# Decoder block on one core: gate recurrence between two heads, PEER routing kept on VectorE, fused W-block instructions, last V products by column halves

## The chip, the core and the metric

One core of a Trainium2 chip runs the whole kernel. Engines are named as in the profile: PE (TensorE matmul) and PEld (its weight load), DVE (VectorE), ACT (ScalarE), POOL (GpSimd) and SP (SyncE, which here only issues DMAs). The metric is the device time of one execution in microseconds, the median of the runs shown.

## What is computed

One decoder layer over 512 tokens of width 1024, in float32 (one layer, one batch):

```python
h = rmsnorm(x, norm1_w) * (1 + sc1) + sh1            # modulated by c @ ada_w
qa, ka, va, qm, km, vm, om, ip, fp, ga, gm = split(h @ w_in)
y_a = diff_attention(rope(qa), rope(ka), va, ...)    # 8 heads
hm  = mlstm_chunkwise(conv(qm), conv(km), vm, ip, fp)  # 8 heads, stabilised gates
merged = sigmoid(ga) * y_a + sigmoid(gm) * (rmsnorm(hm) * sigmoid(om))
x  = x + gt1 * (merged @ w_out)
h2 = rmsnorm(x, norm2_w) * (1 + sc2) + sh2
# PEER: 8 heads, each with two half queries against 128 keys
v_top, i_top = top_k(q @ sub_keys, 16)               # both halves
cand = v_top[0][:, None] + v_top[1][None, :]         # 16 x 16
sc, sel = top_k(cand, 16); idx = (i_top[0] * 128 + i_top[1])[sel]
y = sum_e softmax(sc)[e] * gelu(U[idx[e]] . h2) * V[idx[e]]    # 16384 experts
x = rmsnorm(x + gt2 * y, final_norm_w)
```

Only candidates (i, j) with (i+1)(j+1) <= 16 can be among the best 16, so each head has 50 candidates in rows of 16, 8, 5, 4, 3, 2, 2, 2 and eight single ones (`PAIRS`, `NC` = 50).

## The kernel before

Float32 products are made of three float32r products, hi*hi, hi*lo and lo*hi: `split` (L135) rounds on ACT and subtracts on DVE or POOL, and every weight goes through it.

**Mixers** (`attention`, L443, `mlstm`, L513, called from the loop over four head pairs at L667). A head pair's projections are PE work with two PSUM banks (`acc`); attention of its two heads follows, then `mlstm`, with the projections of `om`, `gm` and `ga` around them. For the first pair `gate_chain` (L331) stands between `attention` and `mlstm`: the running sums and running maxima of the gates of all heads (`tensor_tensor_scan` on DVE, L347 and L349, in 8 partitions), three Exp on ACT (L355 to L357), bf16 thirds copied by ACT and POOL (L363, L364), and the transposes that give `RT`. Its tiles `M` and `iw` lie in the ring `t2k` of three buffers, which rope and attention's output `oT` use too.

**Routing** (from L710). Token tile 0 (`GB`) goes by gathers, tiles 1 to 3 (`DBS`) densely. `scores(h)` projects one head's queries and takes the top 16 of each half (`top16`, five DVE instructions). `select` (L772) works on four heads of one token tile. Its old form builds the candidate sums `cand` on DVE and the candidate indices `cidx` on POOL, takes their top 16, and then finds each pick's index head by head: a 16x50 comparison `eq` on DVE (L797), its product `oh` with `cidx` on POOL (L799), a sum on DVE (L800). `slots` (L816) transposes indices and gates and splits an index into its two key numbers. `build_w` (L833) makes, for 8 tokens at a time (48 blocks), two one-hot tiles and two gated tiles of 128x1024 in float16 with the helper `each` (L843), all on DVE but for the last gated tile of every eighth block, which POOL makes (`PLO`); 16 float16 matmuls (L852, L853) then give the block of W, which ACT evacuates and writes to DRAM.

**Dense loop** (from L984). For key row n1, `up(n1)` (L961) loads a 128x1024 block of U (SP), rounds it (ACT), makes its low part at L967 (POOL for n1 < 35, DVE from there), and runs 24 matmuls (L975 to L977); the result waits in one of 32 `ga` buffers (`NGA`). The loop then multiplies by W (L1006), splits, and runs 18 matmuls against the V block (L1021) into six PSUM banks `ys[d][j]`, d the token tile and j the column half. The last three blocks of V are multiplied together, d by d. In `up`, gathers for token tile 0 are released on POOL behind a small copy, `pace` (L969); `select_gather` runs `select` on its eight heads at n1 = 3 and 5. The end (L1033) scales, adds x, normalises and stores tile by tile.

**What sets the order.** Each engine runs its instructions in one fixed order. It is laid down when the kernel is built, by a scheduler that gives a free engine the ready instruction that stands earliest in the program, and hands out tile buffers as they come free. So the 32 possible `up` calls run ahead into the time in which W is built: they depend on nothing in it, but stand behind it in the program.

Of the kernel before, what the change touches and what calls it, by code (L numbers as in the profile page):

```python
# [61 lines left out]
def block_kernel(ctx: ExitStack, tc: tile.TileContext, a, out, dbg=None):  # L62
# [380 lines left out]
    def attention(hp, y, ssq):  # L443
# [283 lines left out]
    iota_c = dp.tile([P, NC], F16, name="iota_c")  # L727
# [44 lines left out]
    def select(vals, inds, n, mk, didx, dgate):  # L772
# [5 lines left out]
        cidx = mk("cidx", [P, n, NC])  # L778
        for eng, dst, src in ((V, cand, vals), (G, cidx, fi)):
            off = 0  # L780
            for i in range(8):
                m = PAIRS[i]
                eng.tensor_tensor(dst[:, :, off:off + m], src[:, 1, :, 0:m],
                                bc(src[:, 0, :, i:i + 1], [P, n, m]), op=OP.add)
                off += m
            eng.tensor_tensor(dst[:, :, off:off + 8], src[:, 0, :, 8:16],
                            bc(src[:, 1, :, 0:1], [P, n, 8]), op=OP.add)
# [21 lines left out]
    def mk_rp(name, shape, dt=F32):  # L809
        return rp.tile(shape, dt, tag=name, bufs=2, name=name)  # L810
# [298 lines left out]
```

## Time and profile before

| | us |
|---|---|
| median of 3 runs (1979.67 to 1980.06) | 1979.73 |
| the profiled execution | 1986.29 |
| its span, first to last instruction | 1984.2 |
| PE, PEld, DVE, ACT, POOL busy in the span | 1826.5, 1648.0, 1465.3, 806.8, 861.2 |

The busy time of an engine counts overlapping instructions once. Matmuls are pipelined, so that the time of one is longer than the distance to the next. In the views by stretch, PEclk is the granted clock of PE as a share of its higher level, 2.4 GHz (the lower is 1.2 GHz). Mixers end near 640 us, scores run to about 770 us, W is built from 808 to 1005 us, the dense loop ends at 1972 us.

### The profile page before, as it was taken

How to read it: one execution, taken by the hardware profiler on the slowest of the kernel's cores; microseconds unless marked ns; L12 is line 12 of the kernel's file. 1: busy time of each engine (PE TensorE's matmuls, PEld its weight loads, DVE VectorE, ACT ScalarE, POOL GpSimd, SP SyncE). 2: the span in 40 equal slices, each digit the busy share in tenths (PEclk: the TensorE clock that was granted, in tenths of full speed). 3: DMA queues.
4: the chain of work that ended last, by engine and by line, in shares of the span. 5: the costliest groups of instructions: out<-in, count | busy, mean ns of one | idle time of the engine just before them, and what ended most of it. 6: DMA issues, size and time to landing. Idle time of an engine off the chain costs nothing.

```text
span 1984.2 us, 29045 instructions
## 1 busy us (share of the span) xinstructions
PE 1826.5 (92%) x10748; PEld 1648.0 (83%) x10748; DVE 1465.3 (74%) x2740; ACT 806.8 (41%) x1361; POOL 861.2 (43%) x721
## 2 busy tenths in 40 slices
PE   5989999899997988778899989999999999999997
PEld 4979899798986877678888778889988888888986
DVE  7653646546557799998999878888777677767777
ACT  4545464464553323344444333333333333332332
POOL 2513425234234256675533556555433423333433
PEclk8999999999998999899899999999999999999998
DMA  7321414324223222255596699999978888887983
GB/s 278 123 64 60 149 65 154 113 67 139 64 86 107 86 90 81 85 183 202 203 312 215 216 331 339 334 345 348 337 253 296 293 283 291 288 299 234 320 290 129
DMA packets 160284, 404.27 MB, mean 204 GB/s; under 512 B 14471, under 2 KB 63368, under 8 KB 160142
## 3 DMA queue, kind: packets, MB, share of 16 engines
q1 hardware_dynamic: 117026, 240.91, 37.2%
q0 software_dynamic: 36864, 134.23, 18.6%
q10 hardware_dynamic: 6252, 27.28, 3.6%
q8 instruction: 84, 1.38, 0.3%
q14 instruction: 58, 0.48, 0.1%
HBM read 373.52 MB, written 28.84 MB: 203 GB/s over the span
## 4 chain that ended last, share of the span: by engine, by line
PE 51%; DVE 23%; DMA 10%; issue 6%; POOL 5%; ACT 4%; SPq 0%; DVEq 0%; POOLq 0%; ACTq 0%
PE y L1021 18%; PE act L977 5%; PE act L975 5%; PE act L976 5%; DMA ada_w<-ada_w 4%; DMA gath<-V,idx 3%; DVE onehot L844 3%; DVE gated L844 2%; DVE lo_V L138 1%; DVE lo_U L967 1%; DVE eq L797 1%; DMA gath<-U,idx 1%; POOL gath L901 1%; DVE idxf L800 1%; ACT hi_U L966 1%
## 5 line engine op out<-in xcount | busy, mean ns | idle before, releaser
L977 PE MATMUL act<-h_hi,lo_U 128*128 128x384 f32 x1024 | 353.9, 346 | 14.7 <-POOL lo_U L967 9.7
L975 PE MATMUL act<-h_hi,hi_U 128*128 128x384 f32 x1024 | 351.5, 343 | 1.9 <-ACT ga L979 1.9
L976 PE MATMUL act<-h_lo,hi_U 128*128 128x384 f32 x1024 | 350.7, 342 | 0.0
L917 DVE SCALAR_TENSOR_TENSOR yg<-gath,act,yg 128x1024 f32<-128x1024 f32 x127 | 162.9, 1283 | 110.3 <-DMA gath<-V,idx 109.6
L1021 PE MATMUL y<-lo_V,ahi 128*128 128x512 f32 x762 | 238.9, 394 | 5.5 <-DVE lo_V L138 5.5
L1021 PE MATMUL y<-hi_V,alo 128*128 128x512 f32 x762 | 234.1, 394 | 4.0 <-DVE alo L138 4.0
L1021 PE MATMUL y<-hi_V,ahi 128*128 128x512 f32 x762 | 222.1, 396 | 7.3 <-ACT hi_V L137 7.3
L901 POOL DMA_INDIRECT gath<-U,idx x128 | 176.6, 1380 | 115.3 <-DVE junk L907 101.1
L137 ACT CAST hi_V<-raw_V 128x1024 fp32r<-128x1024 f32 x128 | 134.1, 1051 | 225.6 <-PE y L1021 197.1
L977 PEld LDWEIGHTS act<-h_hi,lo_U 128*128 128x128 f32 x1024 | 197.0, 192 | 22.4 <-POOL lo_U L967 11.1
L969 POOL COPY pace<-lo_U 128x1 f32<-128x1 f32 x128 | 69.9, 548 | 331.6 <-DVE lo_U L967 330.1
L975 PEld LDWEIGHTS act<-h_hi,hi_U 128*128 128x128 f32 x1024 | 197.8, 193 | 10.8 <-ACT ga L979 3.1
L976 PEld LDWEIGHTS act<-h_lo,hi_U 128*128 128x128 f32 x1024 | 197.5, 193 | 3.6
L137 ACT CAST ahi<-ga 128x384 fp32r<-128x384 f32 x127 | 65.1, 513 | 302.2 <-DVE ga L1006 152.1
L138 DVE TENSOR_TENSOR lo_V<-raw_V,hi_V 128x1024 fp32r<-128x1024 f32 x128 | 158.0, 1236 | 33.2 <-ACT hi_V L137 30.6
L966 ACT CAST hi_U<-raw_U 128x1024 fp32r<-128x1024 f32 x128 | 134.1, 1048 | 110.0 <-PE act L976 92.3
L1021 PEld LDWEIGHTS y<-hi_V,alo 128*128 128x128 f32 x762 | 143.5, 189 | 35.9 <-DVE alo L138 5.2
L1021 PEld LDWEIGHTS y<-lo_V,ahi 128*128 128x128 f32 x762 | 142.7, 189 | 36.7 <-DVE lo_V L138 7.9
L1021 PEld LDWEIGHTS y<-hi_V,ahi 128*128 128x128 f32 x762 | 143.0, 190 | 32.1 <-ACT hi_V L137 8.0
L901 POOL DMA_INDIRECT gath<-V,idx x128 | 152.5, 1192 | 38.0 <-issue 30.2
L907 DVE SCALAR_TENSOR_TENSOR junk<-gath,hrow 128x1024 bf16<-128x1024 f32 x128 | 156.1, 1220 | 11.9 <-DMA gath<-U,idx 11.2
L967 POOL TENSOR_TENSOR lo_U<-raw_U,hi_U 128x1024 fp32r<-128x1024 f32 x35 | 105.0, 3001 | 72.5 <-ACT hi_U L966 59.1
(461 smaller groups left out, 4413.1 us busy)
## 6 DMA issues: line engine op xcount, KB each, us to landing
raw_U<-UT SPq DMA_DIRECT2D x128, 512.0 KB, 5.1
raw_V<-V SPq DMA_DIRECT2D x128, 512.0 KB, 5.0
ada_w<-ada_w SPq DMA_DIRECT2D x96, 256.0 KB, 4.0
W_dram<-st ACTq DMA_DIRECT2D x24, 960.0 KB, 4.5
W<-W_dram SPq DMA_DIRECT2D x60, 384.0 KB, 10.4
raw_wq<-wq SPq DMA_DIRECT2D x16, 512.0 KB, 3.5
raw_q<-w_in SPq DMA_DIRECT2D x8, 512.0 KB, 4.9
raw_k<-w_in SPq DMA_DIRECT2D x8, 512.0 KB, 3.6
```

The costliest lines, as they stand in the source:

```text
L137: A.copy(hi, src)
L138: eng.tensor_tensor(lo, src, hi.bitcast(F32), op=OP.subtract)
L844: eng.tensor_tensor(dst.rearrange("p t (n u) -> p t n u", u=2), x.rearrange("p t (n u) -> p t n u", u=2), bc(y[:, b * TB:(b + 1) * TB, Non ...
L901: G.indirect_dma_start(out=t_, out_offset=None, in_=src, in_offset=bass.IndirectOffsetOnAxis(ap=idx0[:, s:s + 1], axis=0))
L907: V.scalar_tensor_tensor(junk2, u, 1.0, hrow, op0=OP.mult, op1=OP.mult, accum_out=act[:, s:s + 1])
L917: V.scalar_tensor_tensor(yg, v, act[:, s:s + 1], yg, op0=OP.mult, op1=OP.add)
L966: A.copy(hi, raw)
L967: (G if n1 < NGA + 3 else V).tensor_tensor(lo, raw, hi.bitcast(F32), op=OP.subtract)
L975: T.matmul(ps, hi[:, ks], h_hi[:, k], start=(k == 0), stop=False)
L976: T.matmul(ps, hi[:, ks], h_lo[:, k], start=False, stop=False)
L977: T.matmul(ps, lo[:, ks], h_hi[:, k], start=False, stop=(k == KD - 1))
L1021: T.matmul(ys[d][j], l[:, tsl], r[:, j * 512:(j + 1) * 512], start=(m == 0 and i == 0), stop=(m == KEYS - 1 and i == 2))
```

## The change

- `gate_chain` is called at the start of the second head of the first pair, between the two heads, instead of behind `attention`.
- `select` no longer uses POOL. The 50 candidate positions are decoded into row and column without a table of 50: a float16 comparison of each position with the 16 row starts (`off_c`), products with the differences of the row indices and of the row starts, one sum over both, and a second comparison and sum for the column. Four heads share each instruction. It returns the two key numbers apart, so that `slots` needs no shift and mask; it transposes three tiles instead of two.
- `build_w` makes both one-hot tiles of a block in one instruction, and both gated tiles in another (128x2048 each), always on DVE.
- The low parts of all U blocks are made on DVE.
- In the last V products, each token tile first runs all products of column half 0, then those of half 1.

```diff
-    def attention(hp, y, ssq):
+    def attention(hp, y, ssq, between=None):
...
         for u in range(2):
+            if u and between:
+                between()
...
-        attention(hp, y_a, ssq[:, 0])
-        if hp == 0:
-            gate_chain()
+        attention(hp, y_a, ssq[:, 0], gate_chain if hp == 0 else None)
...
+    n21T = rp.tile([P, XT // TB, 2, TB, 2], F16, name="n21T")
+    ghl = rp.tile([P, XT // TB, 2, TB, 2], F16, name="ghl")
...
+    iota_rep = bc(iota16[:, None, :], [P, 2 * TB, KEYS])
+    V.tensor_copy(iota_c, jcol[:, 0:TOPK])
+    for i in range(TOPK):
+        G.memset(off_c[:, i:i + 1], float(OFFS[i]))
+        G.memset(doff_c[:, i:i + 1], float(OFFS[i] - OFFS[max(i - 1, 0)]))
...
-        fi = mk("fi", [P, 2, n, TOPK])
-        A.activation(fi[:, 0], inds[:, 0], AF.Copy, scale=float(KEYS))
-        A.copy(fi[:, 1], inds[:, 1])
+        ij = mk("ij", [P, 2, n, TOPK], F16)
+        A.copy(ij, inds)
+        di = mk("di", [P, n, TOPK], F16)
+        V.tensor_copy(di[:, :, 0:1], ij[:, 0, :, 0:1])
+        V.tensor_tensor(di[:, :, 1:], ij[:, 0, :, 1:], ij[:, 0, :, :TOPK - 1], op=OP.subtract)
...
-        for h in range(n):
-            eq, oh = mk("eq", [P, TOPK, NC], F16), mk("oh", [P, TOPK, NC])
-            sh = [P, TOPK, NC // 2, 2]
-            V.tensor_tensor(eq.rearrange("p k (c u) -> p k c u", u=2), bc(pos2[:, h, :, None, :], sh),
-                            bc(iota_c.rearrange("p (c u) -> p c u", u=2)[:, None], sh), op=OP.is_equal)
-            G.tensor_tensor(oh, eq, bc(cidx[:, h, None, :], [P, TOPK, NC]), op=OP.mult)
-            V.tensor_reduce(didx[:, h], oh, axis=AX.X, op=OP.add)
+        sh = [P, n * TOPK, TOPK // 2, 2]
+        sh4 = [P, n, TOPK, TOPK]
+
+        def each_pos(dst, table, op):
+            V.tensor_tensor(dst.rearrange("p q (c u) -> p q c u", u=2), bc(pos2[:, :, None, :], sh),
+                            bc(table.rearrange("p (c u) -> p c u", u=2)[:, None], sh), op=op)
+
+        def of_head(dst, src, table):
+            V.tensor_tensor(dst.rearrange("p (h k) c -> p h k c", h=n), src.rearrange("p (h k) c -> p h k c", h=n),
+                            bc(table[:, :, None, :], sh4), op=OP.mult)
+        ge = mk("ge", [P, n * TOPK, TOPK], F16)
+        st = mk("stp", [P, 2 * n * TOPK, TOPK], F16)
+        two = mk("two", [P, 2, n * TOPK])
+        each_pos(ge, off_c, OP.is_ge)
+        of_head(st[:, 0:n * TOPK], ge, di)
+        V.tensor_tensor(st[:, n * TOPK:], ge, bc(doff_c[:, None, :], [P, n * TOPK, TOPK]), op=OP.mult)
+        V.tensor_reduce(two.rearrange("p a q -> p (a q)"), st, axis=AX.X, op=OP.add)
+        V.tensor_copy(dn1, two[:, 0].rearrange("p (h k) -> p h k", k=TOPK))
+        V.tensor_tensor(pos2, pos2, bc(two[:, 1, :, None], [P, n * TOPK, 2]), op=OP.subtract)
+        eq = mk("ge", [P, n * TOPK, TOPK], F16)
+        each_pos(eq, iota_c, OP.is_equal)
+        of_head(eq, eq, ij[:, 1])
+        V.tensor_reduce(dn2, eq.rearrange("p (h k) c -> p h k c", h=n), axis=AX.X, op=OP.add)
...
-            each(e2, iota_rep, n2T, OP.is_equal)
-            each(e1, iota_rep, n1T, OP.is_equal)
-            each(r_hi, e1, ghi, OP.mult)
-            each(r_lo, e1, glo, OP.mult, G if b % 8 < PLO else V)
+            V.tensor_tensor(pairs[0].rearrange("p a t (n u) -> p (a t) n u", u=2),
+                            iota_rep.rearrange("p t (n u) -> p t n u", u=2),
+                            bc(n21T[:, b].rearrange("p a t u -> p (a t) u")[:, :, None, :], [P, 2 * TB, KEYS // 2, 2]),
+                            op=OP.is_equal)
+            V.tensor_tensor(pairs[1].rearrange("p a t (n u) -> p a t n u", u=2),
+                            bc(e1.rearrange("p t (n u) -> p t n u", u=2)[:, None], [P, 2, TB, KEYS // 2, 2]),
+                            bc(ghl[:, b][:, :, :, None, :], [P, 2, TB, KEYS // 2, 2]), op=OP.mult)
...
-        (G if n1 < NGA + 3 else V).tensor_tensor(lo, raw, hi.bitcast(F32), op=OP.subtract)
+        V.tensor_tensor(lo, raw, hi.bitcast(F32), op=OP.subtract)
...
+            steps = [(j, m, i, l, r) for m, ahi, alo, vhi, vlo in vparts
+                     for i, (l, r) in enumerate(((ahi, vhi), (ahi, vlo), (alo, vhi))) for j in range(2)]
+            if n1 == KEYS - 1:
+                steps.sort(key=lambda s: s[0])
+            for j, m, i, l, r in steps:
+                T.matmul(ys[d][j], l[:, tsl], r[:, j * 512:(j + 1) * 512],
+                         start=(m == 0 and i == 0), stop=(m == KEYS - 1 and i == 2))
```

## Rows read from the trace of the kernel before

**Rows 1.** The page: busy us, share of the span, instructions of each engine.
```profile
PE 1826.5 (92%) x10748; PEld 1648.0 (83%) x10748; DVE 1465.3 (74%) x2740; ACT 806.8 (41%) x1361; POOL 861.2 (43%) x721
```
**Rows 2.** Stretches: us, busy (x) of PE, PEld, DVE, ACT, POOL; PEclk, DMA share, GB/s.
```profile
130.00:160.00 30.00, 17.59 (x83) 14.25 (x84) 17.09 (x45) 16.52 (x39) 5.09 (x4) 0.72 0.12 40
...
690.00:808.00 118.00, 98.70 (x482) 86.90 (x482) 111.44 (x573) 40.25 (x73) 72.38 (x92) 0.94 0.28 87
808.00:1005.00 197.00, 163.00 (x1333) 153.21 (x1332) 182.65 (x217) 85.37 (x144) 119.59 (x61) 0.91 0.52 183
1005.00:1200.00 195.00, 183.79 (x884) 160.03 (x882) 172.43 (x410) 70.95 (x101) 89.40 (x77) 0.98 0.80 269
1200.00:1950.00 750.00, 740.03 (x3671) 663.86 (x3670) 565.47 (x680) 259.37 (x355) 331.10 (x305) 1.00 0.86 300
```
**Rows 3.** Waits of PE in the whole span: for whom, us, times, longest.
```profile
PE wps L852 <- DVE gated L844: 17.0, 8, 5.2
...
PE pt_gm L187 <- ACT om L682: 6.6, 1, 6.6
```
**Rows 4.** One stretch, one line each: L844 (DVE, POOL), L797 (DVE), L783 (DVE, POOL).
```profile
690.00:1005.00 315.00, 166.53 (x186) 15.69 (x6) 0.92 0.43 147
...
690.00:1005.00 315.00, 24.13 (x24) 0.92 0.43 147
...
690.00:1005.00 315.00, 12.43 (x48) 9.41 (x48) 0.92 0.43 147
```
**Rows 5.** DVE's timeline: start, us, what.
```profile
802.41 0.57 DVE L797 TENSOR_TENSOR eq<-pos,iota_c 128x800 f16<-128x800 f16 x1
802.89 0.21 DVE L805 TENSOR_REDUCE esm<-ex 128x4 f32<-128x64 f32 x1
...
843.88 2.88 DVE L844 TENSOR_TENSOR onehot<-iota,n2T 128x1024 f16<-128x1024 f16 x1
...
859.67 0.68 DVE L844 TENSOR_TENSOR gated<-onehot,ghi 128x1024 f16<-128x1024 f16 x1
860.27 0.68 DVE L844 TENSOR_TENSOR gated<-onehot,glo 128x1024 f16<-128x1024 f16 x1
...
1043.60 1.13 DVE L783 TENSOR_TENSOR s<-room 128x64 f32<-128x64 f32 x8
```
**Rows 6.** POOL's timeline at the same time as DVE's long one-hot.
```profile
843.32 2.89 POOL L967 TENSOR_TENSOR lo_U<-raw_U,hi_U 128x1024 fp32r<-128x1024 f32 x1 [1.12 <-ACT hi_U L966]
```
**Rows 7.** Lines L967 and L800: ns min/median/max, first and last start us, form.
```profile
L967 DVE TENSOR_TENSOR lo_U<-raw_U,hi_U x93: 1199/1222/1228, 1040.4 to 1945.0; 128x1024 fp32r<-128x1024 f32 x93
...
L967 POOL TENSOR_TENSOR lo_U<-raw_U,hi_U x35: 2340/2562/8862, 751.1 to 1014.3; 128x1024 fp32r<-128x1024 f32 x35
...
L800 DVE TENSOR_REDUCE idxf<-oh x24: 958/970/980, 722.3 to 873.6; 128x16 f32<-128x800 f32 x24
```
**Rows 8.** Stretches, line L976 alone (8 matmuls of each up call): PE, PEld.
```profile
690.00:808.00 118.00, 21.60 (x60) 12.82 (x61) 0.94 0.28 87
808.00:1005.00 197.00, 69.01 (x190) 39.22 (x190) 0.91 0.52 183
```
**Rows 9.** PE's timeline within one up call.
```profile
826.88 0.33 PE L976 MATMUL act<-h_lo,hi_U 128*128 128x384 f32 x1
827.05 0.34 PE L977 MATMUL act<-h_hi,lo_U 128*128 128x384 f32 x1
```
**Rows 10.** The gate recurrence: DVE's and ACT's timelines.
```profile
141.65 0.46 DVE L349 TENSOR_TENSOR_SCAN M<-Gr,mprev 8x128 f32<-8x128 f32 x1
...
149.58 0.61 ACT L355 ACTIVATE iw<-iw 8x512 f32<-8x512 f32 x1
...
152.13 1.08 ACT L682 ACTIVATE om<-pt_om 128x512 f32<-128x512 f32 x2
```
**Rows 11.** The end: PE's last product and DVE's last instruction.
```profile
1971.19 0.63 PE L1021 MATMUL y<-hi_V,ahl 128*128 128x512 f32 x2
...
1979.30 1.41 DVE L1046 SCALAR_TENSOR_TENSOR W<-W,ssq,fw 128x512 f32<-128x512 f32 x2 [0.66 <-POOL ssq L119]
```

More of the change, by code (lines that the diff above doesn't have):

```diff
@@ L37 @@
 NC = sum(PAIRS)
+OFFS = [sum(PAIRS[:i]) for i in range(TOPK)]
 PIECES = [c for hp in range(4) for c in (
@@ L726, in block_kernel @@
     jcol = dp.tile([P, KEYS], I32, name="jcol")
-    iota_c = dp.tile([P, NC], F16, name="iota_c")
+    off_c, doff_c, iota_c = [dp.tile([P, TOPK], F16, name=n) for n in ("off_c", "doff_c", "iota_c")]
     w0pool = ctx.enter_context(tc.tile_pool(name="w0", bufs=1, side="right"))
@@ L770, in scores, with select @@
         A.dma_start(s0_dram[:, h], s0)
-    def select(vals, inds, n, mk, didx, dgate):
-        fi = mk("fi", [P, 2, n, TOPK])
-        A.activation(fi[:, 0], inds[:, 0], AF.Copy, scale=float(KEYS))
-        A.copy(fi[:, 1], inds[:, 1])
-        cand = mk("cand", [P, n, NC])
[L778 to L787, printed above, removed]
+    def select(vals, inds, n, mk, dn1, dn2, dgate):
+        ij = mk("ij", [P, 2, n, TOPK], F16)
[3 more added lines that the diff above has]
+        V.tensor_tensor(di[:, :, 1:], ij[:, 0, :, 1:], ij[:, 0, :, :TOPK - 1], op=OP.subtract)
+        cand = mk("cand", [P, n, NC])
+        off = 0
+        for i in range(8):
+            m = PAIRS[i]
+            V.tensor_tensor(cand[:, :, off:off + m], vals[:, 1, :, 0:m], bc(vals[:, 0, :, i:i + 1], [P, n, m]), op=OP.add)
+            off += m
+        V.tensor_tensor(cand[:, :, off:off + 8], vals[:, 0, :, 8:16], bc(vals[:, 1, :, 0:1], [P, n, 8]), op=OP.add)
         sc = mk("scs", [P, n, TOPK])
@@ L809, in mk_rp @@
     def mk_rp(name, shape, dt=F32):
[L810 removed]
+        return rp.tile(shape, dt, tag=name, bufs=1 if name == "stp" else 2, name=name)
     def select_dense(t, h0, n):
         hs = slice(h0, h0 + n)
[L814 removed]
+        select(vals[t][:, :, hs], inds[t][:, :, hs], n, mk_rp, *[picks[t][:, i, hs] for i in range(3)])
     def slots(t):
[L818 removed]
+        bs = slice((t - DBS[0]) * P // TB, (t - DBS[0] + 1) * P // TB)
         ps = tr_tile("slots")
[L820 to L831 removed]
+        for i in range(3):
+            T.transpose(ps[:, i * P:(i + 1) * P], picks[t][:, i].rearrange("p h k -> p (h k)"), ident)
+        for i in range(2):
+            src = ps[:, i * P:(i + 1) * P].rearrange("p (b t) -> p b t", t=TB)
+            V.tensor_copy(n21T[:, bs, 1 - i], bc(src[:, :, :, None], [P, P // TB, TB, 2]))
+        gp = bc(ps[:, 2 * P:3 * P].rearrange("p (b t) -> p b t", t=TB)[:, :, :, None], [P, P // TB, TB, 2])
+        V.tensor_scalar(ghl[:, bs, 0], gp, GS, None, op0=OP.mult)
+        V.scalar_tensor_tensor(ghl[:, bs, 1], gp, GS, ghl[:, bs, 0], op0=OP.mult, op1=OP.subtract)
     def build_w(t):
[L836 removed]
         for b in range((t - DBS[0]) * P // TB, (t + 1 - DBS[0]) * P // TB):
@@ L926, in mk @@
             n = int(np.prod(shape[1:])) * (2 if dt == F16 else 4) // 4
[L927 removed]
+            if name in ("ge", "stp"):
                 t_, n0 = gpool.tile([P, D], F32, tag="g", bufs=NGB, name=name), 0
[L929 to L930 removed]
+            elif name == "cand":
+                t_, n0 = s0, 0
             else:
@@ L1017, in block_kernel @@
             tsl = slice(d * P, (d + 1) * P)
-            for m, ahi, alo, vhi, vlo in vparts:
-                for i, (l, r) in enumerate(((ahi, vhi), (ahi, vlo), (alo, vhi))):
-                    for j in range(2):
-                        T.matmul(ys[d][j], l[:, tsl], r[:, j * 512:(j + 1) * 512],
-                                 start=(m == 0 and i == 0), stop=(m == KEYS - 1 and i == 2))
+            steps = [(j, m, i, l, r) for m, ahi, alo, vhi, vlo in vparts
[5 more added lines that the diff above has]
+                         start=(m == 0 and i == 0), stop=(m == KEYS - 1 and i == 2))
         vparts = []
```

38 lines of the change are left out of this document (7 added, 31 removed).

## The prediction

> **What bounds the kernel now.** First the page's busy shares: PE is the busiest engine over the span, 92%, DVE second with 74% [rows 1]. The shares are means over stages, so I read the busy times by stretch next [rows 2]. From 1200 to 1950 us PE is busy 740 of 750 us at a granted clock of 1.00: there only less PE work would help, and the change removes none. Three places are different. From 690 to 1005 us PE is busy 98.7 + 163.0 = 261.7 of 315 us, at a clock of 0.94 and 0.91, while DVE is busy 111.4 + 182.7 = 294.1: this stage waits for DVE. From 130 to 160 us PE is busy 17.6 of 30 us at 0.72. And the end: PE's last product ends at 1971.8 us, DVE's last instruction at 1980.7 [rows 11], 9 us in which PE has nothing to do. Then the waits of PE say what ends the idle time: 17.0 us for gated tiles of W, 6.6 us in a single wait for `om` [rows 3]. So the question for each part is how much PE idle time it takes out, and how much PE work it pushes later.
>
> **W stage: why DVE is slow there.** The 186 one-hot and gated instructions on DVE take 166.5 us [rows 4], 0.90 us each. One undisturbed has 0.68 us, and the next starts 0.60 us after it; one at 843.88 takes 2.88 us, and POOL's lo_U runs from 843.32 for 2.89 us [rows 5, 6]. At 0.60 us the 186 would need 112 us: 55 us are lost while POOL computes. The change takes from POOL all that it computes in this stage but the small copies: lo_U, oh, cidx, the gated tiles.
>
> **The sum for DVE, 690 to 1005 us.** I use the distance to the next start, since durations overlap by 0.08 us.
> - W: 96 fused instructions of 2048 elements. 800 elements take 0.48 us to the next start and 1024 take 0.60 [rows 5], so 2048 take 0.60 + 1024 x 0.12/224 = 1.15 us, if the fused form keeps that rate; 110.4 us in place of 166.5: -56.1. Fusing itself gives only 2 x 0.60 - 1.15 = 0.05 us an instruction; the rest is POOL's absence.
> - lo_U: 35 move from POOL to DVE, which makes the other 93 in 1.22 us [rows 7], 1.14 to the next start: +39.9 (a few fall behind 1005 us).
> - Select, six dense groups: old, 24 comparisons in 24.1 us [rows 4] and 24 sums of 0.97 us [rows 7], 47.4 us, or 43.5 without overlaps. New per group: five float16 instructions of 1024 elements at 0.60 = 3.0; four small ones at 0.2, as the reduction of 64 elements (0.21 us) [rows 5]; two sums. A sum of 800 float32 takes 0.97 us [rows 7] and one of 64 0.21 [rows 5], that is 0.00103 us an element, so 1024 take 1.12 and 2048 2.17 us to the next start. Together 7.1 us, 42.6 for six: -1.
> - The candidate sums: 12.4 us for six groups [rows 4], against 1.13 us a group later in the trace [rows 5]: -5.6.
>
> In all -56.1 + 39.9 - 1 - 5.6 = **-23 us** of DVE. Of the sums over float16 no row exists: at the rate of the float16 comparisons they would be 1.15 and 0.60 us, 9 us less over six groups; I take the float32 rate, since it is the same operation, and keep 9 us for the lower end. The Trainium skill (VectorE: DVE Perf Modes, "The perf-mode tier table (the rule you actually need)") says that tensor_reduce has only the one-element mode, whatever the type; by that rule the stage stays at -23, by the other rate it would be -32. No row before shows which.
>
> The stage shortens by less than DVE's 23 us: PE needs 262 of the 315 us, and the two wait for each other block by block. With 17 us gone PE would be 88% busy, still under its 99% in the dense loop. I take **-17**, with 0 and -32 as bounds.
>
> What else moves: oh and cidx on POOL vanish; nothing waits for POOL there then but the pace copies. 32 memsets of one column go to POOL ahead of the scores, hidden in its idle time (72 of 118 us busy from 690 on [rows 2]); without that cover some 0.2 us each, taken from the nearest small DVE row, 6 us, and select alone would wait. A third transpose for each of three token tiles replaces shift and mask: nothing. The two selects for gathers, from 1005 to 1200 us, cost DVE about the same as before; DVE is 88% busy there [rows 2], and PE's dense products hide it. No DMA is added, and SP's queue is as before.
>
> **Gate recurrence.** The first running maximum starts at 141.65 us, right behind the second head's last split, and the Exps that need it (149.58) stand on ACT ahead of the sigmoid of `om` (152.13) [rows 10]. That sigmoid frees the PSUM bank for which `gm`'s projection waits 6.6 us [rows 3]. Called between the heads, the chain stands earlier on both queues, and `om`'s sigmoid need no longer queue behind it. Between 130 and 160 us PE does 17.6 x 0.72 = 12.7 us of full-clock work, so at most 17.3 us can be won (the clock, between its levels of 1.2 and 2.4 GHz here, fell after PE's waits). Against that, 16 short and 2 longer DVE instructions, about 6 us, now stand in front of the second head's maxima, and whoever waits for these, Exp, transposes and value products, starts later; PE has `om`, `gm` and `ga` to fill in. I take **-10**, bounds -17 and +6.
>
> **The end.** Half 0 of the last token tile is complete nine products earlier: 0.17 us for 384 columns [rows 9] makes 0.23 for 512, so 2 us, and its scaling, addition and square run beside half 1's products. I take **-2**, bounds -3 and 0.
>
> **Sum.** -17 - 10 - 2 = -29 us. The profiled execution took 1986.29 us, 6.6 above the median of 1979.73; I subtract from the median: 1951 us.
>
> **Rivals.**
> - *The up calls starve (slower).* lo_U now stands in DVE's queue behind W, which is earlier in the program. 250 matmuls of eight a call [rows 8] say that 31 up calls are done by 1005 us, 24 of them since 808. Each one fewer costs PE later 24 matmuls at 0.17 us [rows 9] = 4.1 us, and relieves DVE by 1.14: net 3.0. From ten fewer on all gains are gone; 18 fewer give 1951 + 54 = 2005 us. For it: DVE is the full engine, and W feeds it without a break. Against it: the index sums of the later token tiles ran until 873.6 us [rows 7], among W's blocks, though they stand behind W's first 16 blocks in the program, so W left room. Chance 0.14.
> - *DVE's time is won, the stage's is not.* If PE and DVE wait for each other in turn, only the 6 us of candidate sums ahead of W remain: 1979.7 - 6 - 12 = 1962 us. For it: PE waits 17.0 us in eight waits [rows 3], few for so long a stage; against it, 55 us of lost DVE time lie on a chain that PE waits for. Chance 0.2.
> - *The recurrence delays the second head:* +6 for -10, 1967 us. Chance 0.1.
> - *The fused instruction does not keep its rate*, because of its wider broadcast. At lo_U's rate (1.14 for 1024) 2048 elements take 2.2 us, 96 x 1.05 = +101: about 2050 us. Against it: pairs of equal values stay the innermost dimension, as in the rows at 0.68. Chance 0.03.
>
> **The numbers.** The forecast has 0.53: 1951 us, its own range 1932 to 1958. A measurement of this kernel tells about 0.2%, 4 us, from no change. Faster: 0.53 + 0.2 + 0.1 less 0.02 = 0.81; within 4 us 0.03, a starving of about ten calls; slower 0.16. For the range, all lower bounds together give -32 - 17 - 3 = -52, 1928, and 3 more for the clock that W's stage would get back: 1925. Upwards it takes in both half gains and the mild starving, to 1982; beyond lie some 0.13 of starving and the lost rate, below 0.04.
>
> **What would show it.** Right: in the W stage the DVE rows at 1.15 to 1.25 us for 2048 elements with no long ones, lo_U on DVE among them, about 30 up calls done when the last block of W is, and that moment 15 to 25 us earlier. PE's wait for `om` gone, and the stretch from 130 to 160 us full at clock 1.00. The last DVE instruction 6 to 7 us after PE's last product in place of 9. Wrong: up calls bunched behind W's last block, W's instructions over 2 us, or PE idle for the second head's maxima near 130 us.

## The result and the profile after

The changed kernel takes 1932.1 us (1931.4 to 1935.7) against 1979.9: a ratio of 0.976 [0.974, 0.978], 47.8 us less. The forecast was 1951, so the direction was right and the gain too small by 19 us. The time is inside the range, at the lower edge of the forecast's own 1932 to 1958.

The page of the profile after, busy time of each engine, beside [rows 1]:

```profile
PE 1814.8 (94%) x10751; PEld 1632.7 (85%) x10751; DVE 1430.7 (74%) x2700; ACT 812.5 (42%) x1359; POOL 691.2 (36%) x608
```

POOL lost 170 us of work; DVE, which took over the larger part of it (lo_U and gated rows), is 35 us *less* busy. The stretches show where. First the same columns as in [rows 2] for the gates and for the whole routing and W stage, from the first query product of the router to the last W block; then its last two parts:

```profile
130.00:160.00 30.00, 26.04 (x201) 23.85 (x200) 16.92 (x28) 22.58 (x44) 12.52 (x8) 1.00 0.23 75
...
625.00:959.00 334.00, 309.17 (x2185) 283.90 (x2185) 310.27 (x906) 151.44 (x258) 77.75 (x82) 0.96 0.47 160
...
812.00:931.00 119.00, 119.00 (x1069) 114.85 (x1067) 115.22 (x117) 67.96 (x115) 38.09 (x21) 1.00 0.67 234
931.00:960.00 29.00, 17.10 (x193) 14.90 (x192) 26.82 (x24) 16.25 (x28) 9.07 (x1) 0.76 0.69 260
```

The same stage of the kernel before, in the same view:

```profile
637.00:1006.00 369.00, 312.86 (x2120) 285.31 (x2120) 336.91 (x951) 146.88 (x258) 208.71 (x163) 0.92 0.41 139
```

The stage went from 369 to 334 us, and PE's idle time in it from 56.1 to 24.8. It also holds more work now. The groups of PE, the third product of each up call (8 a call), before and after:

```profile
L977 PE MATMUL act<-h_hi,lo_U 128*128 128x384 f32 x251 | 92.8, 370 | 9.7 <-POOL lo_U L967 9.7
```
```profile
L994 PE MATMUL act<-h_hi,lo_U 128*128 128x384 f32 x272 | 93.7, 345 | 2.5 <-DVE lo_U L984 2.5
```

That is 31 calls by the last W block before, 34 after; the mean of one product fell from 370 to 345 ns as the granted clock rose from 0.92 to 0.96. From 812 to 931 us PE is full at 1.00, where it was busy 163.0 of 197 us at 0.91 before [rows 2]; from 931 on it has no up call left (34 is all that there is room for, 32 in `ga` buffers and two in PSUM banks) and waits for W.

PE's waits in the stage before (us, times, longest), beside the 17.0 us of [rows 3]:

```profile
PE act L977 <- POOL lo_U L967: 9.7, 5, 4.3
PE slots L820 <- DVE idxf L800: 6.0, 1, 6.0
PE wps L853 <- POOL gated L844: 5.2, 2, 3.6
PE pkeys L764 <- DVE scr L749: 4.9, 1, 4.9
PE wps L853 <- DVE gated L844: 4.2, 5, 1.8
```

And what is left after:

```profile
PE wps L868 <- DVE gated L863: 10.0, 9, 2.5
PE act L992 <- ACT ga L996: 5.2, 3, 2.8
PE act L994 <- DVE lo_U L984: 2.5, 3, 0.9
```

DVE's groups in that stage after (busy us and mean ns, then the idle time ahead of them):

```profile
L859 DVE TENSOR_TENSOR onehot<-iota,n21T 128x2048 f16<-128x2048 f16 x48 | 57.5, 1217 | 2.7 <-PE wps L869 2.4
L863 DVE TENSOR_TENSOR gated<-onehot,ghl 128x2048 f16<-128x2048 f16 x48 | 57.4, 1215 | 0.1
L984 DVE TENSOR_TENSOR lo_U<-raw_U,hi_U 128x1024 fp32r<-128x1024 f32 x36 | 43.6, 1212 | 1.4 <-ACT hi_U L983 1.1 <-issue 0.2
...
L815 DVE TENSOR_REDUCE two<-stp 128x128 f32<-128x2048 f16 x6 | 13.6, 2264 | 0.0
...
L821 DVE TENSOR_REDUCE picks<-ge 128x64 f32<-128x1024 f16 x6 | 7.2, 1201 | 0.0
```

None of these means is more than 0.02 us above what the forecast took for an undisturbed instruction; before, the first one-hot alone had 1067 ns for 1024 elements, and DVE waited 12.6 us for PE ahead of it:

```profile
L844 DVE TENSOR_TENSOR onehot<-iota,n2T 128x1024 f16<-128x1024 f16 x48 | 51.0, 1067 | 12.6 <-PE wps L853 12.6
```

**Where the time went.** Three marks cut every execution: Q, the start of the second head pair's first query product; W, the end of the last W block; and the end of the span. This table holds for all that follows (medians with lowest and highest; ratios, with 95% intervals, to runs of the kernel before that were measured beside each kernel; the last three columns from the profiled execution):

| kernel | us | ratio | to Q | Q to W | W to end |
|---|---|---|---|---|---|
| before | 1979.9 | 1 | 180 | 826 | 978 |
| after | 1932.1 (1931–1936) | 0.976 [0.974, 0.978] | 167 | 791 | 971 |
| after, gates back | 1953.5 (1950–1955) | 0.987 [0.984, 0.990] | 180 | 788 | 981 |
| after, lo_U on POOL | 1938.8 (1936–1940) | 0.979 [0.976, 0.983] | 168 | 802 | 968 |
| after, four instructions | 1926.6 (1921–1933) | 0.974 [0.971, 0.978] | 165 | 795 | 960 |
| after, POOL work ahead of W | 1951.5 (1949–1953) | 0.985 [0.982, 0.989] | 170 | 812 | 970 |
| before, gates moved | 1970.3 (1965–1975) | 0.996 [0.993, 0.998] | 165 | 826 | 977 |
| before, lo_U to DVE | 1961.5 (1958–1965) | 0.992 [0.990, 0.994] | 181 | 804 | 975 |
| after, POOL work beside W | 1972.8 (1968–1977) | 0.998 [0.996, 1.000] | 166 | 833 | 968 |
| after, old column order | 1932.9 (1927–1937) | 0.978 [0.973, 0.983] | 169 | 792 | 969 |
| after, old select | 1943.6 (1940–1954) | 0.983 [0.978, 0.988] | 165 | 801 | 972 |
| after, 35 buffers | 1914.3 (1913–1919) | 0.966 [0.962, 0.970] | 169 | 795 | 953 |
| the same, four instructions | 1921.4 (1919–1923) | 0.970 [0.966, 0.974] | 169 | 802 | 949 |
| 35 buffers, row tile on DVE | 1911.3 (1907–1916) | 0.965 [0.959, 0.970] | 168 | 790 | 947 |

Between the two profiled executions the change is -13, -35 and -7 us, 55 together. The profiled execution of before lies 6.4 us above its median and that of after 0.8 below, which leaves the 47.8 of the medians. In which part the 6.4 us lie isn't shown; Q to W has the same 826 us in the run with the gates moved, whose profiled execution lies at its median. To Q, executions differ by up to 5 us in themselves (165 to 170 with the same code), and from W to the end kernels with the same code there by about 20 (960 to 981 among those with 34 up calls by W).

### The profile page after: what moved, and what is told of

The parts are those of the page before. It is cut to its first block, busy times and chain, and to the rows that moved or that the text cites. A ratio compares the mean times of both kernels' runs of the same rounds, so it can differ in the third digit from the quotient of the medians.

```text
span 1929.6 us, 28881 instructions
## 1 busy us (share of the span) xinstructions
PE 1814.8 (94%) x10751; PEld 1632.7 (85%) x10751; DVE 1430.7 (74%) x2700; ACT 812.5 (42%) x1359; POOL 691.2 (36%) x608
## 4 chain that ended last, share of the span: by engine, by line
PE 63%; DVE 16%; DMA 8%; ACT 5%; issue 5%; POOL 3%; SPq 0%; DVEq 0%; POOLq 0%; ACTq 0%
PE y L1040 23%; PE act L994 7%; PE act L992 7%; PE act L993 7%; DMA ada_w<-ada_w 4%; DMA gath<-V,idx 2%; DVE lo_U L984 1%; DVE ada_acc L219 1%; DVE lo_V L138 1%; DVE ga L699 1%; PE wps L868 1%; PE wps L869 1%; ACT p L489 1%; PE pr_wq L187 1%; PE pr_wq L188 1%
## 5 line engine op out<-in xcount | busy, mean ns | idle before, releaser
L994 PE MATMUL act<-h_hi,lo_U 128*128 128x384 f32 x1024 | 346.8, 339 | 8.1 <-DVE lo_U L984 8.1
L992 PE MATMUL act<-h_hi,hi_U 128*128 128x384 f32 x1024 | 345.6, 337 | 6.1 <-ACT ga L996 5.2
L993 PE MATMUL act<-h_lo,hi_U 128*128 128x384 f32 x1024 | 344.4, 336 | 0.0
L986 POOL COPY pace<-lo_U 128x1 f32<-128x1 f32 x128 | 100.2, 784 | 572.1 <-DVE lo_U L984 571.9
L1040 PE MATMUL y<-lo_V,ahi 128*128 128x512 f32 x762 | 242.9, 398 | 4.1 <-DVE lo_V L138 4.1
L917 POOL DMA_INDIRECT gath<-U,idx x128 | 172.6, 1348 | 127.0 <-DVE junk L923 112.6
L994 PEld LDWEIGHTS act<-h_hi,lo_U 128*128 128x128 f32 x1024 | 192.8, 188 | 16.1 <-DVE lo_U L984 11.3
L992 PEld LDWEIGHTS act<-h_hi,hi_U 128*128 128x128 f32 x1024 | 193.0, 188 | 11.6 <-ACT ga L996 6.2
L993 PEld LDWEIGHTS act<-h_lo,hi_U 128*128 128x128 f32 x1024 | 192.7, 188 | 4.0
L984 DVE TENSOR_TENSOR lo_U<-raw_U,hi_U 128x1024 fp32r<-128x1024 f32 x128 | 156.0, 1219 | 20.9 <-ACT hi_U L983 15.6
```

The costliest lines, as they stand in the source:

```text
L917: G.indirect_dma_start(out=t_, out_offset=None, in_=src, in_offset=bass.IndirectOffsetOnAxis(ap=idx0[:, s:s + 1], axis=0))
L984: V.tensor_tensor(lo, raw, hi.bitcast(F32), op=OP.subtract)
L986: with tc.issue_after(G.tensor_copy(pace, lo[:, 0:1].bitcast(F32)).ins):
L992: T.matmul(ps, hi[:, ks], h_hi[:, k], start=(k == 0), stop=False)
L993: T.matmul(ps, hi[:, ks], h_lo[:, k], start=False, stop=False)
L994: T.matmul(ps, lo[:, ks], h_hi[:, k], start=False, stop=(k == KD - 1))
```

## The experiments

**The gates, undone in the changed kernel.**

```diff
-        attention(hp, y_a, ssq[:, 0], gate_chain if hp == 0 else None)
+        attention(hp, y_a, ssq[:, 0])
+        if hp == 0:
+            gate_chain()
```

> The changed kernel with one part undone: the gate recurrence stands behind the whole first attention again. Theory (my step of 10 us is right, and the landmarks of the two traces agree: the second head pair's first query product starts at 165 us in place of 180, the third's at 295 in place of 307.5): about 1942 us, between 1938 and 1946. Rival 1, the recurrence is only hidden differently and the later stages take its 10 us back: 1932 us. Rival 2, the part of the gain that my sum did not have (19 us) came from here: 1955 us or more.

1953.5 us: 21 more, a miss, and close to what rival 2 said. PE's stretch and its wait are those of before again:

```profile
130.00:160.00 30.00, 17.46 (x84) 14.39 (x84) 15.89 (x45) 17.14 (x38) 4.95 (x4) 0.72 0.13 40
```
```profile
PE pt_gm L187 <- ACT om L684: 6.6, 1, 6.6
```

But the marks put only 12 us at the gates, and by the middle of the V products 8 are left (1390 against 1382 us). Another 10 appear from W to the end, where the same lines run in both. Hence the counterpart, **the gates alone in the kernel before** (the same edit the other way):

> The kernel before with one part of the change: the gate recurrence between the heads, nothing else. Undoing this part in the changed kernel cost 21 us, of which the trace places 8 to 12 at the gates and up to half of the V products (1390 against 1382 us), and the rest in the second half of the dense loop, where no line was changed. Theory (the part is worth about 10 us where it stands; the rest is the order in which DVE's queue of the dense loop comes out, another in each kernel): the first query product of the second head pair 11 to 13 us earlier, half of the V products 8 to 12 us earlier, the total 1962 to 1974 us. Rival (the part itself is worth 20 us, and shows itself late): 1955 to 1961 us, with the second half of the V products shorter than before's 548 us by 8 or more.

1970.3 us, a gain of 8 (3 to 13 by the interval). The stretch:

```profile
130.00:160.00 30.00, 27.43 (x200) 25.27 (x199) 16.39 (x28) 22.08 (x42) 10.06 (x7) 0.94 0.22 75
```

PE is about as busy as after (26.04 us, at 1.00); 15 us earlier at Q, the same from Q to W. So the part is worth about what the forecast gave it, and the further 10 us of the first run are not its own. The two programs' DVE queues do differ in the dense loop (the gathered rows' sums stand in other places among lo_V and alo), because the order is planned over the whole program. That this order costs the 10 us fits, and was not tried by itself.

**lo_U back on POOL.**

```diff
-        V.tensor_tensor(lo, raw, hi.bitcast(F32), op=OP.subtract)
+        (G if n1 < NGA + 3 else V).tensor_tensor(lo, raw, hi.bitcast(F32), op=OP.subtract)
```

> The changed kernel with one part undone: lo_U of the first 35 up calls is POOL's again. Theory (what POOL computes beside DVE slows DVE, and a lo_U of 2.9 us is late for PE): DVE is rid of 35 x 1.14 = 40 us, but its fused instructions become long ones of 2.5 to 3 us beside each lo_U, some 55 us lost; PE's waits for lo_U (9.7 us before) are back and its granted clock in the W stage falls under 0.95. Together 1950 to 1972 us. Rival (the gain came from the fused instructions and the new select, and lo_U on DVE is a price paid for nothing): DVE 40 us freer, 1905 to 1930 us.

1938.8 us: less than expected, and its interval touches that of after. The stage says more than the total. DVE's groups among the W blocks, and POOL's:

```profile
L863 DVE TENSOR_TENSOR gated<-onehot,ghl 128x2048 f16<-128x2048 f16 x47 | 82.7, 1793 | 0.1
L859 DVE TENSOR_TENSOR onehot<-iota,n21T 128x2048 f16<-128x2048 f16 x45 | 68.7, 1559 | 1.9 <-PE wps L869 1.8
```
```profile
L984 POOL TENSOR_TENSOR lo_U<-raw_U,hi_U 128x1024 fp32r<-128x1024 f32 x23 | 64.6, 2807 | 76.7 <-ACT hi_U L983 73.0 <-ACT W L874 3.7
```

DVE was rid of 36 instructions, 41 us, and yet was busy 327.6 us in the stage in place of 310.3: 58 us lost beside POOL's 35. The stage took 348 us in place of 334. The rival, DVE freer by 40 and a faster kernel, is out. PE's waits for lo_U did not come back (3.0 us), nor did DVE's idle time (348 - 327.6 = 20.4 us): only the contention did, without the late products.

**The other direction: lo_U and the gated rows to DVE, alone in the kernel before.**

```diff
-PLO = 1
+PLO = 0
...
-        (G if n1 < NGA + 3 else V).tensor_tensor(lo, raw, hi.bitcast(F32), op=OP.subtract)
+        V.tensor_tensor(lo, raw, hi.bitcast(F32), op=OP.subtract)
```

> The kernel before with one part of the change: the 35 lo_U and the low gated rows of one W block in eight go from POOL to DVE; the select, the four instructions a block and the gates stay. POOL keeps the select's products (32 + 14 us), most of them ahead of the W blocks. Theory (POOL's absence beside W is the gain of the W stage): one-hot and gated instructions at 0.68 us, first to last W block 150 to 160 us in place of 187, the total 1950 to 1965 us. Rival (the gain is in the fused instructions and the new select): DVE has 40 us more to do and nothing in return, 1985 us or more.

1961.5 us, as the theory said; the blocks took 163 us from first to last, a little over the expected 160, and 188 before. The stage and one of the four groups of one-hot and gated rows:

```profile
634.00:986.00 352.00, 317.25 (x2186) 287.91 (x2184) 330.75 (x994) 153.11 (x265) 109.56 (x128) 0.95 0.45 152
```
```profile
L844 DVE TENSOR_TENSOR gated<-onehot,ghi 128x1024 f16<-128x1024 f16 x48 | 32.8, 683 | 0.1
```

This run decides most. DVE's busy time hardly fell (336.9 to 330.8: the 41 us of lo_U ate what the shorter rows gave back), but the stage is 17 us shorter and holds 34 up calls in place of 31. What went is idle time of both: PE's from 56.1 to 34.8, DVE's from 32.1 to 21.3. Of PE's waits it is not those for lo_U that went: 8.9 us are left, now for DVE's. Those for W's rows went from 17.0 + 5.2 + 4.2 = 26.4 to 7.7 + 3.5 = 11.2, that for `slots` (6.0) wholly, and DVE's for PE from 12.6 to 4.8:

```profile
PE act L977 <- DVE lo_U L967: 8.9, 6, 2.7
PE wps L852 <- DVE gated L844: 7.7, 9, 2.2
```
```profile
DVE onehot L844 <- PE wps L853: 4.8, 9, 1.2
```

In the kernel before, one event makes 7.1 of the 12.6 us and shows how the three engines hung together. POOL's, PE's and DVE's timelines:

```profile
909.65 8.86 POOL L967 TENSOR_TENSOR lo_U<-raw_U,hi_U 128x1024 fp32r<-128x1024 f32 x1 [4.73 <-ACT hi_U L966]
```
```profile
918.56 0.44 PE L977 MATMUL act<-h_hi,lo_U 128*128 128x384 f32 x1 [4.30 <-POOL lo_U L967]
...
920.52 0.53 PE L975 MATMUL act<-h_hi,hi_U 128*128 128x384 f32 x1
```
```profile
923.42 0.69 DVE L844 TENSOR_TENSOR onehot<-iota,n2T 128x1024 f16<-128x1024 f16 x1 [7.11 <-PE wps L853]
```

Beside DVE's one-hot and gated instructions, which followed each other without a gap up to 916.3 us and kept their 0.68, POOL's lo_U took 8.86 us; its median is 2.56 [rows 7]. PE stood 4.30 us for it and did its next products in 0.53 us in place of 0.34 (a granted clock of 0.50 from 919.3 to 922.0 us), and only then came to the W products whose tiles DVE needed back.

**POOL work that nobody waits for.** Behind each of the first 35 up calls' lo_U, POOL subtracts two tiles into one that nobody reads. In the first form it read tiles that were there anyway:

```diff
+        if n1 < NGA + 3:
+            for k in range(2):
+                idle = dp.tile([P, 448], BF16, tag="idle", bufs=1, name="idle")
+                G.tensor_tensor(idle, h2_hi[:, k, 0:448].bitcast(F32), h2_lo[:, k, 0:448].bitcast(F32), op=OP.subtract)
```

> The changed kernel with work added: in each of the first 35 up calls POOL also subtracts 2 x 448 elements of two tiles that lie in SBUF anyway, into a tile that nobody reads, so nobody waits for its result but the pace copies behind it. The output is the reference's. Theory (POOL's computing in itself slows DVE): the fused instructions beside it take 2 to 3 us in place of 1.22, some 35 x 1 to 1.5 us of DVE lost, 1955 to 1985 us. Rival (the long instructions of before were only waits for data, no contention): 1932 us, within 4, and all fused instructions stay at 1.2 us.

1951.5 us, in size as the theory said, but not as it said: with nothing to wait for, all 70 ran ahead of the W blocks, and the fused instructions stayed at 1.22 us. There, among the scores and the first selects, DVE's busy time grew from 170.2 to 193.0 us up to the first W block. The second form reads `lo`, so that it falls where lo_U does:

```diff
-                G.tensor_tensor(idle, h2_hi[:, k, 0:448].bitcast(F32), h2_lo[:, k, 0:448].bitcast(F32), op=OP.subtract)
+                G.tensor_tensor(idle, lo[:, k * 448:(k + 1) * 448].bitcast(F32), h2_lo[:, k, 0:448].bitcast(F32), op=OP.subtract)
```

> The changed kernel with work added, now so that it falls among the W blocks: behind each of the first 35 lo_U of DVE, POOL subtracts 2 x 448 of its elements from another tile, into a tile that nobody reads. The output is the reference's. Without this dependency all of it ran ahead of the W blocks, and cost 21 us there. Theory (POOL's computing slows DVE's two-input instructions beside it): fused instructions of 2 us and more, first to last W block 165 to 185 us in place of 146, the total 1950 to 1970 us. Rival (DVE's instructions are not touched by work that nobody waits for): fused ones all at 1.22, the first to last W block 146 to 150, the total 1932 to 1937 us.

1972.8 us, 40 more than after and a little over the expected 1970. The stage, then DVE's groups in it:

```profile
624.00:1000.00 376.00, 321.26 (x2185) 289.52 (x2185) 357.18 (x906) 153.32 (x259) 171.75 (x152) 0.95 0.42 142
```
```profile
L859 DVE TENSOR_TENSOR onehot<-iota,n21T 128x2048 f16<-128x2048 f16 x48 | 76.9, 1625 | 0.9 <-PE wps L869 0.8
L863 DVE TENSOR_TENSOR gated<-onehot,ghl 128x2048 f16<-128x2048 f16 x48 | 71.3, 1504 | 0.1
...
L815 DVE TENSOR_REDUCE two<-stp 128x128 f32<-128x2048 f16 x6 | 13.6, 2265 | 0.0
...
L756 DVE MAX8 vals<-scr 128x8 f32<-128x128 f32 x24 | 6.6, 276 | 0.0
```

The same 906 DVE instructions took 357.2 us in place of 310.3, beside work whose result nobody reads. POOL's computing in itself slows DVE, and not every instruction: those with two inputs grew, while the sums (2265 ns, 2264 after) and the maxima of a tile in SBUF (276, 273 after) are as they were. Copies within SBUF can grow too: with lo_U on POOL, `di` took 1178 ns in the median (minimum, median, maximum below) where it takes 158 after.

```profile
L783 DVE COPY di<-ij x6: 152/1178/2128, 693.3 to 789.9; 128x4 f16<-128x4 f16 x6
```

The Trainium skill (SBUF — State Buffer, "Who interferes with whom") says that a DVE instruction with two SBUF inputs contends with a GpSimd one that reads SBUF, through a shared read interface, and that tensor_reduce never contends on this chip. The trace agrees, by the numbers just given. By the same page ("SBUF: two separate sides") whichever of the two starts first has the shared ports for its whole instruction; the last section shows both cases (1.12 us for a copy of 0.19, and 4.32 for instructions of 2.35).

**Four instructions in place of two.**

```diff
-            V.tensor_tensor(pairs[0].rearrange("p a t (n u) -> p (a t) n u", u=2),
...
-            V.tensor_tensor(pairs[1].rearrange("p a t (n u) -> p a t n u", u=2),
...
+            each(e2, iota_rep[:, 0:TB], n21T[:, b, 0], OP.is_equal)
+            each(e1, iota_rep[:, 0:TB], n21T[:, b, 1], OP.is_equal)
+            each(r_hi, e1, ghl[:, b, 0], OP.mult)
+            each(r_lo, e1, ghl[:, b, 1], OP.mult)
```

> The changed kernel with one part undone: a W block is made by four instructions of 1024 elements, all on DVE, in place of two of 2048. Theory (fusing gives next to nothing): 192 x 0.60 in place of 96 x 1.15 us is 5 us more of DVE; PE is full from 812 to 931 us, so at most that: 1932 to 1938 us. Rival (fewer, longer instructions are what shortened the stage): half of the stage's gain is gone, 1950 us or more.

1926.6 us, below the expected 1932 to 1938: no difference to after that the intervals can tell. DVE was busy 316.4 us in the stage, 6 more than after, against the 5 worked out, and Q to W grew by 4. W to the end, where no line was changed, came out 11 us shorter, and hides that in the total.

**The old select and index transposes.** The functions `select` and `slots` and their calls are those of before; W's tables keep the new layout.

> The changed kernel with one part undone: the select and the index transposes of before, with their products and index sums on POOL; the gates, lo_U on DVE, the fused instructions and the column halves stay. The gates alone gave 8 us and lo_U with the gated rows 16 us, together 24 of 48; fusing and the columns gave nothing. Theory (the rest is the select, because POOL's products slow DVE and W's blocks wait for a chain that goes DVE, POOL, DVE for each head): 1948 to 1958 us, first to last W block 155 to 165 us in place of 146, and the first block later. Rival 1 (my step: the new select frees DVE of 1 us and the candidate sums of 5.6): 1935 to 1941 us. Rival 2 (the parts only win together, the select has no share of its own): 1932 us, within 4.

1943.6 us, 11.5 more, between theory and rival 1. From the first W block to the last it took 154 us in place of 145, but the first came hardly later in the stage (190 us from its start, 188 after). The stage, and one of W's two instructions:

```profile
621.00:966.00 345.00, 312.67 (x2188) 287.03 (x2186) 324.44 (x898) 152.28 (x262) 122.12 (x128) 0.95 0.45 155
```
```profile
L846 DVE TENSOR_TENSOR onehot<-iota,n21T 128x2048 f16<-128x2048 f16 x48 | 60.5, 1280 | 3.7 <-PE wps L856 3.5
```

DVE is busy 14 us more than after, where the sum's two terms for the select had 1 + 5.6. POOL's products stood not only beside the candidate sums: W's two instructions and lo_U took 168.6 us here and 158.5 after.

Alone, the gates gave 8 us and lo_U with the gated rows 16; the old select cost 11.5. That is 36 of the 48. The other 12 have no run of their own.

**The old order of the last V products.**

```diff
-            if n1 == KEYS - 1:
-                steps.sort(key=lambda s: s[0])
```

> The changed kernel with one part undone: the last V products go column half by column half within each step again. Theory (the order brings nothing, since at the end DVE is full with the three earlier row tiles): from PE's last product to DVE's last instruction 9 us as in both traces, the total 1932 us, within 4. Rival (my step: the order hides 2 us, and the trace of after only shows another delay in its place): the gap grows to 11 us, the total 1934 to 1938 us.

1932.9 us: nothing in the total. The end of this run, PE's last product and DVE's last instruction:

```profile
1916.71 0.63 PE L1038 MATMUL y<-hi_V,ahl 128*128 128x512 f32 x2
```
```profile
1926.15 1.42 DVE L1063 SCALAR_TENSOR_TENSOR W<-W,ssq,fw 128x512 f32<-128x512 f32 x2 [0.66 <-POOL ssq L119]
```

And of after, PE, POOL and DVE:

```profile
1916.97 0.40 PE L1040 MATMUL y<-hi_V,ahl 128*128 128x512 f32 x1
```
```profile
1907.08 3.87 POOL L1059 TENSOR_TENSOR yg<-yg,x 128x512 f32<-128x512 f32 x1 [10.86 <-DVE yg L1058]
```
```profile
1912.77 1.42 DVE L1065 SCALAR_TENSOR_TENSOR yg<-yg,ssq,fw 128x512 f32<-128x512 f32 x2 [0.69 <-POOL ssq L119]
...
1925.14 1.41 DVE L1065 SCALAR_TENSOR_TENSOR W<-W,ssq,fw 128x512 f32<-128x512 f32 x2 [0.66 <-POOL ssq L119]
```

From PE's end to DVE's: 1917.34 to 1927.57, 10.2 us, with the old order; 1917.37 to 1926.55, 9.2, with the new. So in this pair the new order wins 1 us. Against the 8.9 of before it's lost again to a later start of DVE's closing part, 4.6 us ahead of PE's end in place of 6.0; POOL's addition took 3.87 us beside DVE's last splits, and 1.66 in before. In three other runs with the new order that addition took 1.67 and the gap is 8.5 us, where the old order has 8.7 to 8.9 (before and its two variants): there it wins some 0.3. In the run with the old select, though, the addition took 1.66 and the gap is 9.3, so the addition alone does not set it.

**Room for more up calls.** PE had no call left from 931 us on, so the activations got 35 buffers; the space comes from tiles that only DVE uses.

```diff
-NGA = 32
+NGA = 35
...
-        return rp.tile(shape, dt, tag=name, bufs=1 if name == "stp" else 2, name=name)
+        return rp.tile(shape, dt, tag=name, bufs=1 if name in ("stp", "ge", "two", "di", "cand", "scr2") else 2, name=name)
```

> The changed kernel with room for three more up calls ahead of the first V product: 35 activation buffers in place of 32; the SBUF space comes from five tiles of the select that only DVE writes and reads, held once in place of twice. In the changed kernel the 34th up call ends at 931 us, and until the last W block at 960 PE is busy 17 of 29 us at a granted clock of 0.76. Theory (PE is out of up calls there, and DVE sets the end): three calls of 24 x 0.17 = 4.1 us fill that hole, DVE does 3 x 1.14 us more, net 3 x 3.0 = 9 us: 1923 us, between 1918 and 1927. Rival 1 (the W blocks wait for lo_U and end later by as much as PE wins): 1932 us, within 4. Rival 2 (the tiles held once make the select wait): 1936 us or more.

1914.3 us: 18 less than after, twice the expected 9. Up calls at 957 us, by their third product:

```profile
L994 PE MATMUL act<-h_hi,lo_U 128*128 128x384 f32 x296 | 100.7, 341 | 2.1 <-DVE lo_U L984 2.1
```

These are 37 calls. The stage grew by 4 us (DVE's three lo_U), and W to the end fell by 18, more than the three calls' 12.2 us of products. What the rest is stays open. With four instructions a block:

> The same with room for three more up calls, and W's blocks made by four instructions of 1024 elements again, all on DVE, as in the run that undid the fusing (1926.6 us, 1921 to 1933, against 1932). Theory (fusing brings nothing, and the instruction count of DVE does not matter here): the same time as with the two long instructions, within 5 us. Rival (four short instructions are better, because a lo_U or a candidate sum comes in between sooner): 4 us or more faster than with the two.

1921.4 us, 7 more than with two, beyond the 5 that the theory allowed: of the four times of each only one pair overlaps (1918.9 here, 1919.1 there). Q to W is 7 us longer too, and DVE 6 us busier in the stage (321.15 against 314.70). So in both pairs four instructions lengthen the stage, by 4 and 7 us, about what their work on DVE comes to. Last, the end once more, on the version with 35 buffers:

```diff
-            (V, G)[1 - j].tensor_tensor(y[:, js], y[:, js], xr[:, js], op=OP.add)
+            (V if t == GB else (V, G)[1 - j]).tensor_tensor(y[:, js], y[:, js], xr[:, js], op=OP.add)
```

> The version with 35 activation buffers, with one more edit at the end: both halves of the residual addition of the gathered row tile run on DVE, in place of one on POOL. In the changed kernel that addition took POOL 3.87 us beside DVE's last splits, and DVE's closing instructions, which stand behind it in the queue, began 4.6 us ahead of PE's last product where the kernel before began 6.0 ahead. Theory (the column halves do win 1 us, 10.2 to 9.2 us from PE's last product to DVE's last instruction, and this late addition holds back the rest of my 2 us): DVE's closing part begins 6 to 8 us ahead of PE's last product, the gap falls to 7 or 8 us, the total 1912 to 1914 us. Rival (DVE's own closing work sets the gap, and one more addition of 0.68 us lengthens it): 9.5 to 10 us, the total the same or 1 us more.

1911.3 us (1907 to 1916), not to be told from 1914.3. PE's last product ends at 1893.95, DVE's last instruction at 1902.62: 8.7 us, against 9.2 in the run with 35 buffers, and DVE's closing part begins 5.1 us ahead of PE's end in place of 4.6. Both moved the way of the theory, by less than it said; DVE's own closing work sets most of the gap.

## Why the prediction was right and where it fell short

**DVE's sum: right.** W's two instructions take 57.5 + 57.4 us, two in a row 2.35, so 1.14 from one start to the next: 109.4 in place of the 110.4 forecast; 36 lo_U made it 41 us for the 39.9; the select's products and sums are 47.6 us (20.3 + 20.8 + 6.5 of small ones) where the forecast had -1 on 47.4; the sums over float16 ran at 2264 and 1201 ns, the float32 rate that was taken, as the Trainium skill (VectorE: DVE Perf Modes, "The perf-mode tier table (the rule you actually need)") has it. DVE's busy time in the stage fell by 26.6 us, 23 forecast.

**"The stage shortens by less than DVE's 23 us [...] I take -17": the step that failed.** The stage shortened by 35, beyond the lower bound of 32, with three more up calls in it. Of the 35 us, 26.6 are DVE's busy time, about the sum, and 8.4 its idle time (32.1 to 23.7 us). The reason given for a discount was that PE and DVE wait for each other block by block. That is so, and counts the other way: with POOL's work gone, DVE waits less for PE ahead of W's one-hots (12.6 to 2.4 us), and PE less for W's rows (26.4 to 10.0). The event at 909.65 us shows how POOL came into it, and the run that moved only lo_U and the gated rows won some 21 us from Q to W while DVE had 6 us less to do. Which part of POOL's work caused how much of the idle time stays open: lo_U put back alone did not bring DVE's back (20.4 us), nor did the old select (345 - 324.4 = 20.6).

**"3 more for the clock": small in the forecast.** The stage's PE work went from 312.86 us for 2120 products, 147.6 ns each, to 309.17 for 2185, 141.5 each: 6.1 x 2185 = 13 us of PE time, at a granted clock of 0.92 and 0.96. How much this shortened the stage isn't shown. DVE's busy time makes 26.6 of the 35 us, so a quicker PE can have added no more than the 8.4 by which DVE's idle time fell. The clock had a place in the range alone, though [rows 2] showed 0.94 and 0.91 over 315 us.

**The select: its share stood in two terms.** Its own instructions cost DVE what was forecast. Undoing it cost 14 us of DVE and 11.5 of the total, against the 1 + 5.6 of its own two terms, but 10 of the 14 are W's rows and lo_U beside POOL's products, and W's rows the forecast had among the 55 us lost while POOL computes. The sum was not wrong by this.

**The gates: right in mechanism and size.** -10 forecast, -13 to Q, -8 as a single edit, and 21 lost when it alone was undone, 12 of them to Q. The wait for `om` is gone, and the stretch from 130 to 160 us is at 1.00 with 26.0 us busy.

**The end: -2, and nothing came.** The column halves win 0.3 to 1 us, and the gap is 9.2 us where 6 to 7 were forecast. The step took PE's last products as what DVE waits for; but from 1912.77 us on, before PE ended, DVE was busy with the earlier row tiles' closing work, 12.7 of the 13.8 us to its end.

**The rivals.** The up calls did not starve: 34 by 931 us, where 31 were done by 1005. DVE's time was not lost on the way to the stage; the fused instruction kept its rate. The second head was delayed, as the third rival said, by 9 to 11 us at its maxima; here the last one before and after:

```profile
135.15 1.23 DVE L483 TENSOR_REDUCE nmx<-sc 128x2 f32<-128x1024 f32 x1 [0.52 <-PE sc L481]
```
```profile
146.50 1.20 DVE L485 TENSOR_REDUCE nmx<-sc 128x2 f32<-128x1024 f32 x1
```

It cost nothing, because PE had the projections to do, as the forecast also said: it is busy 26.0 + 30.0 of the 60 us from 130 to 190, and 17.6 + 30.0 before. Left without a term was the dense loop: 7 us between the profiled executions from W to the end. Three up calls fewer are left there, some 12 us of PE, but kernels with the same 34 calls by W lie anywhere from 960 to 981; no claim is made on it.

## What to carry to other kernels

Look at what an engine's work does to the other engines, and not only at how full each one is: work moved from POOL to a fuller DVE paid here, because POOL's two-input work took more from DVE (58 us in one run) than the work itself (41). Where two engines wait for each other in turn, an edit that takes a third out of their way can give more than the fuller engine's saving (here 35 us for 26.6); bound the gain by the stage's idle and slow time, not by that saving. When a stage gets shorter, look at once for what runs out next: here up calls at 931 us, and three more buffers gave another 18 us.

## What was not expected of the hardware

A POOL copy of one element, behind each lo_U, took 0.18 to 0.59 us while DVE did the scores. Among W's blocks ten of the 22 took 1.12 us, nearly as long as the DVE two-input instruction beside them, and five 3.4 to 9.1. POOL's and DVE's timelines of the changed kernel:

```profile
770.00 0.19 POOL L986 COPY pace<-lo_U 128x1 f32<-128x1 f32 x1 [6.21 <-DVE lo_U L984]
...
884.95 1.12 POOL L986 COPY pace<-lo_U 128x1 f32<-128x1 f32 x1 [6.03 <-DVE lo_U L984]
```
```profile
884.80 2.36 DVE L859 TENSOR_TENSOR onehot<-iota,n21T 128x2048 f16<-128x2048 f16 x2
```

The first of the two one-hots runs from 884.80 to about 886.0, the copy until 886.07. The other way round, with lo_U on POOL, DVE's instruction waits for POOL's end:

```profile
863.01 2.38 POOL L984 TENSOR_TENSOR lo_U<-raw_U,hi_U 128x1024 fp32r<-128x1024 f32 x1 [6.95 <-ACT hi_U L983]
```
```profile
863.29 4.32 DVE L859 TENSOR_TENSOR onehot<-iota,n21T 128x2048 f16<-128x2048 f16 x2 [1.59 <-PE wps L869]
```

Two one-hots need 2.35 us; here 4.32, which is 1.97 more, and POOL's lo_U ran for 2.10 us after the first had been due to start. So in these two cases the price of a collision is what is left of the other engine's instruction. Long instructions on POOL are dear to DVE. DVE's rows in turn cost POOL's small copies time that no engine waits for in this stage, but they made lo_U on POOL late in the kernel before (8.86 us at 909.65), and PE waited for that.
